# Twenty short chunks in the state-space scan of a hybrid encoder layer, and a new order of the work around it

## The chip, the core and the metric

One core of a Trainium2 chip runs the whole program in one launch. The metric is device microseconds of one execution, as the median of three runs. A core has five engines with queues of their own: TensorE (PE, matmuls; its weight loads are shown as PEld), VectorE (DVE), ScalarE (ACT), GpSimd (POOL) and SyncE (SP), which here issues nearly all DMAs. Each engine runs its instructions in the order of its queue.

## The reference

One layer of an encoder on 256 + 1024 tokens of width 1024. The input projection feeds three mixers; then come an output projection, a gated MLP, a gated layer embedding and a final norm. The change is about the second mixer, S5: 16 groups of 64 complex states, one recurrence forward and one backward, each from `s_t = a s_(t-1) + B u_t`:

```python
bu_re = jnp.einsum('blgi,gpi->blgp', ug, bb_re)
bu_im = jnp.einsum('blgi,gpi->blgp', ug, bb_im)
_, _, s_re, s_im = lax.associative_scan(
    complex_linear_combine, (a_re, a_im, bu_re, bu_im), reverse=rev, axis=1)
y_dir = jnp.einsum('blgp,gip->blgi', s_re, cr) - jnp.einsum('blgp,gip->blgi', s_im, ci)
```

The first mixer, SSD, is a chunked scan over x, B and C, which a projection, a width-3 convolution and SiLU make (`xbc`); it needs step sizes dt and their running sums (`dt_prep`).

## The kernel before

Everything is kept with features on the 128 partitions and tokens along the free axis. A product in near-float32 is three matmuls of high and low parts; `wload` loads a weight block of 128 columns, ScalarE rounds it (`whi`), and VectorE or GpSimd makes the rest (`wlo`, L70).

*S5.* Eight tokens make one block, so there are 32 + 128 = 160 blocks. `s5_coef` makes the coefficients and their powers up to 8. `s5_fac` makes, for four groups at a time, the factors `v1p` (VectorE, L1085 to L1090), which PE transposes (`ps_v`, L1095) and ScalarE copies out (L1096), and `wc` (GpSimd, L1103 to L1107), both stored to DRAM; 64 small matmuls give the taps inside a block (`ps_k`, L1111). `s5_pow` makes the table Q of the first 32 powers of a^8. `s5_scan` multiplies the factors with the blocks (`ps_w`, L1232; two groups at a time, eight times) and copies the result out of PSUM into S (L1236 to L1239), forward states on partitions 0 to 63, backward ones reversed on 64 to 127. S is [component, 16 groups x 5 chunks, 33]: 160 blocks are five chunks of 32, the first chunk the short sequence. Then the recurrence runs over j = 2 to 32 inside all chunks at once: four instructions a step (L1250 to L1253), VectorE on groups 0 to 10 (2 x 11 x 5 = 110 elements) and GpSimd on groups 11 to 15 (50 elements). The ends of chunks are carried to the next (L1267 and the same four lines), and each block gets the power times the state that enters its chunk: twelve pairs of a product (L1280) and a sum (L1281) on each engine. `s5_taps` stores the taps. `s5_out` copies the states before each block into X (L1304 to L1307, VectorE) and multiplies (`ps_y`, L1318 and L1320).

*What sets the order.* Functions are generators. `xbc` issues 8 projection blocks, each 3 windows of 24 matmuls of about 430 columns (`ps_i`, L468), with a `yield` after every six: 96 steps of some 1.07 us of planned time. `drive` steps the main generator and lets a `Background` go on whenever planned time has passed its own wait; `finish` issues all that is left. That gives the order of issue, which is the priority: a planner with a timeline of its own then lays each engine's queue, taking the first instruction that it holds to be ready. The work on a finished window (`flush`: three VectorE instructions L397, L679 and L681, two of ScalarE, one store) and weight loads get high priority.

Before the change `s5_fac` and `s5_pow` are issued whole, ahead of `xbc`. Then the first 72 steps of `xbc` run with `s5_scan` behind a wait of 16 us and `dt_prep` from the start; the other 24 steps run beside `ssd1` (L1610), which needs the stored x and B and `dt_prep`'s weights; then two z blocks (`gate`, 24 steps) run beside `ssd1` and `s5_out`, and everything of these is finished (L1616) before the other two z blocks. Buffers are stacks of pools: `dt_prep`'s (`dtw`) are on the right side, S (`s5s`) on the left.

Of the kernel before, what the change touches and what calls it, by code (L numbers as in the profile page):

```python
# [1141 lines left out]
def s5_pow(k):  # L1142
    v = k.nc.vector
    t = lambda nm, sh: k.s5w.tile([128] + sh, F32, name="s5_" + nm)

# [7 lines left out]
    Q = k.s5p.tile([128, 2, 32, 16], F32, name="s5_Q")
    v.tensor_copy(out=Q[:, :, 0], in_=k.s5P[:, :, 8])
    TQ = t("TQ", [2, 16, 16])
    for n in (1, 2, 4, 8, 16):
        j = signed(f"qj{n}", Q[:, 1, n - 1])
        bc = lambda a: a.unsqueeze(1).to_broadcast([128, n, 16])
        for c in range(2):
            v.tensor_tensor(out=TQ[:, c, :n], in0=bc(j[:, c]), in1=Q[:, 1 - c, 0:n], op=ALU.mult)  # L1160
            v.tensor_tensor(out=Q[:, c, n:2 * n], in0=bc(Q[:, 0, n - 1]), in1=Q[:, c, 0:n], op=ALU.mult)
        v.tensor_tensor(out=Q[:, :, n:2 * n], in0=Q[:, :, n:2 * n], in1=TQ[:, :, :n], op=ALU.add)
    k.s5q = Q
    k.s5j8 = signed_p(k, Q[:, 1, 0], "s5_j8")
    k.s5j256 = signed_p(k, Q[:, 1, 31], "s5_j256")
# [38 lines left out]
def s5_scan(k):  # L1204
    nc = k.nc
    k.s5xd = k.s5ud.rearrange("t (i g) b -> (t i) g b", g=16)

# [55 lines left out]
    tc_ = k.s5s.tile([128, 2, 2, 16], F32, name="s5_tc")
    sh = [128, 2, 16]
    a256 = Q[:, 0, 31].unsqueeze(1).to_broadcast(sh)
    for c in range(2, 5):
# [564 lines left out]
```

## Time and profile before

| what | us |
|---|---|
| median of 3 runs (1745.33 to 1749.23) | 1746.09 |
| the profiled execution, its own time | 1741.83 |
| its span, first to last instruction | 1740.0 |
| PE busy (94%) | 1633.0 |
| DVE busy (63%) | 1097.3 |
| ACT busy (48%) | 832.4 |
| POOL busy (47%) | 825.3 |
| 84 to 340 us: PE / DVE / POOL busy, of 256 | 229.3 / 236.2 / 116.5 |

Busy time is the time covered by an engine's instructions. Matmuls are pipelined, so a busy PE isn't PE at its peak, and the granted clock has to be read beside it. Most of the span, from 560 us on, is the MLP, where PE is nearly always busy. The stretch of the change is 84 to 340 us.

### The profile page before, as it was taken

Reading aid. Unit: us, or ns where it says so; the run is one execution under the profiler, and the core shown is the slowest. Engines: PE = TensorE matmul, PEld = TensorE weight load, DVE = VectorE, ACT = ScalarE, POOL = GpSimd, SP = SyncE. Lnnn points to the kernel's source line nnn. Section 1 sums busy time; section 2 is a strip of 40 time slices with the busy share of each in tenths; the row PEclk is TensorE's granted clock in tenths of the full one; section 3 lists DMA queues with packets and bytes.
Section 4 is the critical chain, followed back from the end, with each engine's and each line's share of the span. In section 5 each row is a group of like instructions: output and inputs, shape, how many; then the busy total and the mean of one; then the engine's idle time right before and its main releaser. Section 6 shows DMA issues by size and latency. Waiting matters only on the chain.

```text
span 1740.0 us, 27569 instructions
## 1 busy us (share of the span) xinstructions
PE 1633.0 (94%) x10384; PEld 1565.3 (90%) x10384; DVE 1097.3 (63%) x2053; ACT 832.4 (48%) x1363; POOL 825.3 (47%) x514
## 2 busy tenths in 40 slices
PE   6979988999888999999999999999999999999995
PEld 4869976887678998999999999999999999999994
DVE  8996999858698988345755521655543465553255
ACT  5323422167556565545655533555543455554353
POOL 5251575167584655744444444444454434444333
PEclk9989999999988999999999999999999999999997
DMA  6535345797885548755444444444466434444443
GB/s 236 170 139 160 115 131 172 255 298 248 248 266 182 166 147 266 220 184 183 154 134 145 141 136 137 146 145 135 135 191 207 145 126 158 134 145 129 145 142 101
DMA packets 136973, 296.58 MB, mean 170 GB/s; under 512 B 13896, under 2 KB 76296, under 8 KB 136840
## 3 DMA queue, kind: packets, MB, share of 16 engines
q1 hardware_dynamic: 136696, 294.81, 53.1%
q8 instruction: 82, 1.34, 0.3%
q14 instruction: 51, 0.42, 0.1%
q10 hardware_dynamic: 144, 0.00, 0.0%
HBM read 255.02 MB, written 40.80 MB: 170 GB/s over the span
## 4 chain that ended last, share of the span: by engine, by line
PE 66%; DVE 19%; DMA 6%; issue 4%; ACT 2%; POOL 2%; SPq 0%; DVEq 0%; ACTq 0%; POOLq 0%
PE ps_u L78 33%; PE ps_d L271 17%; PE ps_o L78 6%; PE ps_g L78 5%; PE ps_i L468 3%; DMA e<-csd 1%; DVE sgvT L1466 1%; DVE wlo L70 1%; DVE s_S L1252 1%; DMA er<-ecsd 1%; DVE s_S L1253 1%; DVE ic L679 1%; POOL wlo L70 1%; DMA wraw<-in_w_up_dram 1%; DVE ps_i L397 1%
## 5 line engine op out<-in xcount | busy, mean ns | idle before, releaser
L70 POOL TENSOR_TENSOR wlo<-wraw,whi 128x1024 fp32r<-128x1024 f32 (+2 forms) x244 | 583.6, 2394 | 702.1 <-ACT whi L61 699.1
L61 ACT ACTIVATE whi<-wraw 128x1024 fp32r<-128x1024 f32 (+1 forms) x359 | 371.5, 1036 | 420.3 <-issue 170.9
L78 PE MATMUL ps_u<-ahi,whi 128*128 128x342 f32 (+2 forms) x1408 | 440.9, 314 | 7.8 <-DVE cv L186 7.1
L78 PE MATMUL ps_u<-ahi,wlo 128*128 128x342 f32 (+2 forms) x1408 | 438.9, 312 | 0.9 <-POOL wlo L70 0.8
L78 PE MATMUL ps_u<-alo,whi 128*128 128x342 f32 (+2 forms) x1408 | 438.1, 311 | 1.4 <-DVE alo L70 0.8
L78 PEld LDWEIGHTS ps_u<-ahi,whi 128*128 128x128 f32 x1408 | 267.8, 190 | 10.2 <-ACT whi L61 4.9
L78 PEld LDWEIGHTS ps_u<-ahi,wlo 128*128 128x128 f32 x1408 | 269.1, 191 | 2.0 <-POOL wlo L70 1.6
L78 PEld LDWEIGHTS ps_u<-alo,whi 128*128 128x128 f32 x1408 | 268.3, 191 | 2.3 <-DVE alo L70 1.1
L70 DVE TENSOR_TENSOR wlo<-wraw,whi 128x1024 fp32r<-128x1024 f32 (+1 forms) x115 | 144.6, 1258 | 128.8 <-ACT whi L61 128.7
L271 PE MATMUL ps_d<-gh,whi 128*128 128x342 f32 (+2 forms) x704 | 218.8, 311 | 1.2 <-ACT gh L112 1.2
L271 PE MATMUL ps_d<-gh,wlo 128*128 128x342 f32 (+2 forms) x704 | 218.6, 311 | 0.9 <-POOL wlo L70 0.6
L271 PE MATMUL ps_d<-gl,whi 128*128 128x342 f32 (+2 forms) x704 | 218.2, 310 | 0.1
L185 DVE SCALAR_TENSOR_TENSOR cv<-ps_u,c_const,cv 128x341 f32<-128x341 f32 (+2 forms) x176 | 96.3, 548 | 126.6 <-ACT cv L184 126.1
L468 PE MATMUL ps_i<-hi,whi 128*128 128x428 f32 (+5 forms) x408 | 153.7, 377 | 7.8 <-DVE ic L681 4.6
L468 PE MATMUL ps_i<-hi,wlo 128*128 128x428 f32 (+5 forms) x408 | 150.0, 369 | 2.6 <-POOL wlo L70 1.9
L468 PE MATMUL ps_i<-lo,whi 128*128 128x428 f32 (+5 forms) x408 | 150.8, 370 | 0.0
L271 PEld LDWEIGHTS ps_d<-gh,whi 128*128 128x128 f32 x704 | 133.1, 189 | 1.7 <-ACT gh L112 1.4
L271 PEld LDWEIGHTS ps_d<-gh,wlo 128*128 128x128 f32 x704 | 133.3, 190 | 1.3 <-POOL wlo L70 0.8
L271 PEld LDWEIGHTS ps_d<-gl,whi 128*128 128x128 f32 x704 | 133.2, 189 | 0.4 <-DVE gl L70 0.3
L184 ACT ACTIVATE cv<-ps_u,c_const 128x342 f32<-128x342 f32 (+2 forms) x176 | 106.7, 607 | 15.6 <-DVE ps_u L250 15.6
L272 DVE TENSOR_TENSOR x<-ps_d,x 128x342 f32<-128x342 f32 (+2 forms) x32 | 15.7, 492 | 152.1 <-PE ps_d L271 152.1
L186 DVE SCALAR_TENSOR_TENSOR cv<-ps_u,c_const,cv 128x341 f32<-128x341 f32 (+2 forms) x176 | 96.3, 548 | 3.7
(428 smaller groups left out, 2956.5 us busy)
## 6 DMA issues: line engine op xcount, KB each, us to landing
wraw<-in_w_up_dram SPq DMA_DIRECT2D x176, 512.0 KB, 3.3
wraw<-in_w_down_dram SPq DMA_DIRECT2D x64, 512.0 KB, 3.5
wraw<-in_w_out_dram SPq DMA_DIRECT2D x32, 512.0 KB, 3.9
wraw<-in_ple_gate_dram SPq DMA_DIRECT2D x32, 512.0 KB, 3.4
...
```

The lines of the kernel that those rows point to most:

```text
L61: nc.scalar.activation(out=hi[:, :n], in_=raw[:, :n], func=AF.Copy)
L70: eng.tensor_tensor(out=lo, in0=x, in1=hi.bitcast(F32), op=ALU.subtract)
L78: k.nc.tensor.matmul(out=out, lhsT=a, rhs=b, start=(i == 0 and j == 0), stop=(i == n - 1 and j == 2))
L184: nc.scalar.activation(out=c[:, :N], in_=ps[:, :N], func=AF.Identity, scale=cw[:, 1:2], bias=cb)
L185: nc.vector.scalar_tensor_tensor(out=c[:, 1:N], in0=ps[:, 0:N - 1], scalar=cw[:, 0:1], in1=c[:, 1:N], op0=ALU.mult, op1=ALU.add)
L186: nc.vector.scalar_tensor_tensor(out=c[:, 0:N - 1], in0=ps[:, 1:N], scalar=cw[:, 2:3], in1=c[:, 0:N - 1], op0=ALU.mult, op1=ALU.add)
L271: nc.tensor.matmul(out=ps[:, :N], lhsT=a[:, i], rhs=g[f][r][:, :N], start=(f == 0 and j == 0), stop=(f == NF - 1 and j == 2))
L397: k.nc.vector.tensor_tensor(out=ps if out is None else out, in0=ps, in1=k.rstd[:n, a:b], op=ALU.mult)
L468: nc.tensor.matmul(out=ps, lhsT=x[:, i], rhs=k.h[i][y][:, a:b], start=i + n == 0, stop=i == KC - 1 and n == 2)
L679: nc.vector.scalar_tensor_tensor(out=o(s, b), in0=u(s - 1, b - 1), scalar=k.scw[:, j, 0:1], in1=o(s, b), op0=ALU.mult, op1=ALU.add)
L1252: e.tensor_tensor(out=dst, in0=dst, in1=t[:, 0], op=ALU.add)
L1253: e.tensor_tensor(out=dst, in0=dst, in1=t[:, 1], op=ALU.add)
```

## The change

The scan's chunks become 8 blocks long, 20 of them: 4 for the short sequence, 16 for the long one. S becomes [component, 9, 16 groups, 20 chunks], j outside; the recurrence has 7 steps; VectorE takes groups 0 to 11 and GpSimd 12 to 15. The chunk ends are scanned in two levels (within fours, then four times from one four to the next, with the table R of powers of a^64), copied to j = 0, and the correction is made with 8 products and 8 sums for 7 x n x 20 elements, n = 6 twice on VectorE and 4 once on GpSimd. Evictions are two copies an engine instead of three; of X's four VectorE copies one stays and two go to ScalarE. `s5_fac` gets yields and runs, behind a wait of 7 us, beside the first 40 steps of `xbc`, and `dt_prep` behind a wait of 20 us; both are finished there. `s5_pow` follows, `dtw` is closed on the left, where `s5s` is then opened, and `s5_scan` runs beside the next 32 steps without a wait of its own.

```diff
         v.tensor_tensor(out=v1[:, 1], in0=v1[:, 1], in1=tm[:, 1], op=ALU.add)
+        yield 6
...
         nc.sync.dma_start(out=k.s5wc[q4], in_=w)
+        yield 5
...
+    TQ = t("TQ", [2, 4, 16])
+    k.s5q = powers("Q", k.s5P[:, :, 8], 8, TQ)
+    k.s5r = powers("R", k.s5q[:, :, 7], 4, TQ)
+    k.s5j8 = signed_p(k, k.s5q[:, 1, 0], "s5_j8")
...
-    S = k.s5s.tile([128, 2, 80, 33], F32, name="s5_S")
-    k.s5F, k.s5S = S, S.rearrange("p c (g k) j -> p c g k j", g=16)
+
+    S = k.s5S = k.s5s.tile([128, 2, 9, 16, 20], F32, name="s5_S")
...
-            copy(out=S[0:64, c, 5 * g0:5 * g0 + 5 * n, 1:33], in_=src[0:64].rearrange("p g (c j) -> p (g c) j", j=32))
-            o = k.s5S[64:128, c, g0:g0 + n]
-            copy(out=o[:, :, 0, 1:33], in_=src[64:128, :, 31::-1])
-            copy(out=o[:, :, 1:5, 1:33], in_=src[64:128, :, :31:-1].rearrange("p g (c j) -> p g c j", j=32))
+            for h, s in ((0, src[0:64]), (64, src[64:128, :, ::-1])):
+                copy(out=S[h:h + 64, c, 1:9, g0:g0 + n].rearrange("p j g q -> p g q j"), in_=s.rearrange("p g (q j) -> p g q j", j=8))
...
-    parts = ((nc.vector, 0, 11), (nc.gpsimd, 11, 16))
...
-    for j in range(2, 33):
+
+    for j in range(2, 9):
...
+            mac(e, t, S[:, :, j, g0:g1], ar, aj, S[:, :, j - 1, g0:g1])
+
+    E = S[:, :, 8]
+    v = nc.vector
+    t4 = flat[0][:, :320].rearrange("p (i c g q) -> p i c g q", i=2, c=2, q=5)
+    for i in range(1, 4):
+        sh = [128, 2, 16, 5]
+        mac(v, t4, E[:, :, :, i::4], R[:, 0, 0].unsqueeze(1).unsqueeze(3).to_broadcast(sh), jr[:, :, 0].unsqueeze(3).to_broadcast(sh), E[:, :, :, i - 1::4])
+    for m in range(1, 5):
+        p = slice(64 if m == 1 else 0, 64 if m == 4 else 128)
+        sh = [p.stop - p.start, 2, 16, 4]
+        ar = R[p, 0].rearrange("p i g -> p g i").unsqueeze(1).to_broadcast(sh)
+        mac(v, t4[p, :, :, :, 0:4], E[p, :, :, 4 * m:4 * m + 4], ar, jr[p].rearrange("p c i g -> p c g i"), E[p, :, :, 4 * m - 1:4 * m].to_broadcast(sh))
+    v.memset(S[:, :, 0, :, 0:1], 0.0)
+    v.tensor_copy(out=S[:, :, 0, :, 1:20], in_=E[:, :, :, 0:19])
+    v.memset(S[0:64, :, 0, :, 4:5], 0.0)
+    v.memset(S[64:128, :, 0, :, 16:17], 0.0)
+
+    for e, g0, g1 in ((nc.vector, 0, 6), (nc.gpsimd, 12, 16), (nc.vector, 6, 12)):
...
+        sh = [128, 7, n, 20]
+        t = flat[e is nc.gpsimd][:, :140 * n].rearrange("p (j g q) -> p j g q", j=7, q=20)
+        q = [Q[:, m, 0:7, g0:g1].unsqueeze(3).to_broadcast(sh) for m in range(2)]
+        en = [S[:, m, 0, g0:g1].unsqueeze(1).to_broadcast(sh) for m in range(2)]
+        for m, a, b, op in ((0, 0, 0, ALU.add), (0, 1, 1, ALU.subtract), (1, 0, 1, ALU.add), (1, 1, 0, ALU.add)):
+            o = S[:, m, 1:8, g0:g1]
+            e.tensor_tensor(out=t, in0=q[a], in1=en[b], op=ALU.mult)
+            e.tensor_tensor(out=o, in0=o, in1=t, op=op)
...
-        nc.vector.tensor_copy(out=X[0:64].rearrange("p c g (k j) -> p c (g k) j", j=32), in_=k.s5F[0:64, :, 5 * g0:5 * g0 + 10, 0:32])
-        nc.vector.tensor_copy(out=X[64:128, :, :, 31::-1], in_=S[64:128, :, g0:g0 + 2, 0, 0:32])
+        nc.vector.tensor_copy(out=X[0:64].rearrange("p c g (q j) -> p c (g q) j", j=8), in_=S[0:64, :, 0:8, g0:g0 + 2].rearrange("p c j g q -> p c (g q) j"))
         for c in range(2):
-            nc.vector.tensor_copy(out=X[64:128, c, :, :31:-1].rearrange("p g (k j) -> p g k j", j=32), in_=S[64:128, c, g0:g0 + 2, 1:5, 0:32])
+            nc.scalar.copy(out=X[64:128, c, :, ::-1].rearrange("p g (q j) -> p g q j", j=8), in_=S[64:128, c, 0:8, g0:g0 + 2].rearrange("p j g q -> p g q j"))
...
-    s5_fac(k)
+
+    d = ExitStack()
+    open_(d, "dtw", 1)
+    open_(d, "dtw2", 1)
+    g1, g2 = Background(wait(7), s5_fac(k)), Background(wait(20), dt_prep(k))
+    xs = xbc(k)
+    drive(k, islice(xs, 40), g1, g2)
+    finish(g1, g2)
     s5_pow(k)
+    d.close()
     b.close()
     open_(a, "s5s", 1)
     open_(a, "s5o", 2)
-    b = ExitStack()
-    open_(b, "dtw", 1, side="right")
-    open_(b, "dtw2", 1, side="right")
-    g1, g2 = Background(wait(16), s5_scan(k)), Background(dt_prep(k))
-    xs = xbc(k)
-    drive(k, islice(xs, 72), g1, g2)
-    finish(g2)
-    b.close()
+    g1 = Background(s5_scan(k))
+    drive(k, islice(xs, 32), g1)
```

## Rows read from the trace of the kernel before

**Rows 1.** Busy by stretch: start:end length, PE, PEld, DVE, ACT, POOL, clock, DMA.
```profile
84.00:130.00 46.00, 34.64 (x184) 29.91 (x183) 44.74 (x74) 9.90 (x14) 27.85 (x17) 0.85 0.36 128
130.00:200.00 70.00, 70.00 (x385) 65.21 (x383) 55.65 (x165) 27.22 (x54) 11.51 (x14) 1.00 0.47 149
200.00:340.00 140.00, 124.65 (x622) 106.12 (x623) 135.80 (x305) 30.17 (x47) 77.15 (x150) 0.98 0.53 168
```

**Rows 2.** The same for the projection's matmuls (L468) alone: PE, PEld, clock, DMA.
```profile
84.00:200.00 116.00, 69.31 (x320) 61.16 (x319) 0.94 0.43 141
130.00:200.00 70.00, 49.68 (x239) 44.64 (x240) 1.00 0.47 149
200.00:340.00 140.00, 93.63 (x420) 78.42 (x419) 0.98 0.53 168
```

**Rows 3.** Waits of PE, 84 to 340 us: total, times, longest.
```profile
PE ps_v L1095 <- DVE v1p L1089: 10.5, 3, 3.9
...
PE ps_bT L756 <- DVE bT L778: 8.3, 6, 2.4
```

**Rows 4.** DVE's groups of the scan: busy us, mean ns, idle before.
```profile
L1250 DVE TENSOR_TENSOR s_t<-s_Q,s_S 128x110 f32<-128x110 f32 x31 | 11.6, 373 | 0.4
...
L1251 DVE TENSOR_TENSOR s_t<-s_j,s_S 128x110 f32<-128x110 f32 x31 | 13.1, 424 | 0.0
...
L1252 DVE TENSOR_TENSOR s_S<-s_S,s_t 128x110 f32<-128x110 f32 x31 | 16.7, 539 | 0.0
...
L1253 DVE TENSOR_TENSOR s_S<-s_S,s_t 128x110 f32<-128x110 f32 x31 | 14.3, 461 | 0.3
...
L1280 DVE TENSOR_TENSOR s_tE<-s_Q,s_S 128x352 f32<-128x352 f32 x12 | 9.9, 824 | 0.1
...
L1281 DVE TENSOR_TENSOR s_S<-s_S,s_tE 128x352 f32<-128x352 f32 x12 | 8.6, 718 | 0.1
```

**Rows 5.** Instructions on S alone, 181 to 310 us: DVE, ACT, POOL busy.
```profile
181.00:310.00 129.00, 76.38 (x167) 1.78 (x6) 63.82 (x148) 0.97 0.45 143
```

**Rows 6.** Instructions on S: shortest/median/longest ns, first and last start.
```profile
L1250 DVE TENSOR_TENSOR s_t<-s_Q,s_S x31: 342/361/522, 181.5 to 269.0; 128x110 f32<-128x110 f32 x31
...
L1252 DVE TENSOR_TENSOR s_S<-s_S,s_t x31: 299/465/2325, 182.2 to 271.6; 128x110 f32<-128x110 f32 x31
...
L1253 DVE TENSOR_TENSOR s_S<-s_S,s_t x31: 297/365/1450, 182.9 to 273.1; 128x110 f32<-128x110 f32 x31
...
L1280 DVE TENSOR_TENSOR s_tE<-s_Q,s_S x12: 741/774/1028, 274.0 to 308.5; 128x352 f32<-128x352 f32 x12
...
L1281 DVE TENSOR_TENSOR s_S<-s_S,s_tE x12: 508/524/2033, 275.7 to 309.3; 128x352 f32<-128x352 f32 x12
...
L1281 POOL TENSOR_TENSOR s_S<-s_S,s_tE x12: 491/582/847, 275.2 to 297.5; 128x160 f32<-128x160 f32 x12
...
L1307 DVE COPY s5X<-s_S x16: 285/289/292, 307.2 to 337.2; 64x256 f32<-64x256 f32 x16
```

**Rows 7.** Timeline of DVE, alone and beside POOL: start us, us, instruction.
```profile
83.62 1.59 DVE L1087 TENSOR_TENSOR v1p<-s_PW,s_bba 128x512 f32<-128x512 f32 x1
...
102.50 0.69 DVE L1087 TENSOR_TENSOR v1p<-s_PW,s_bba 128x512 f32<-128x512 f32 x1
...
203.19 2.33 DVE L1252 TENSOR_TENSOR s_S<-s_S,s_t 128x110 f32<-128x110 f32 x1
```

**Rows 8.** Timeline of POOL in the last of these moments.
```profile
202.90 2.39 POOL L70 TENSOR_TENSOR wlo<-wraw,whi 128x1024 fp32r<-128x1024 f32 x1
```

**Rows 9.** Timeline of DVE: start and end of `dt_prep`, last eviction.
```profile
155.93 0.33 DVE L595 TENSOR_TENSOR dtx<-ps_dtT,c_const 128x160 f32<-128x160 f32 x1
...
191.68 0.47 DVE L1236 COPY s_S<-ps_w 64x320 f32<-64x320 f32 x1
...
209.54 0.39 DVE L565 TENSOR_TENSOR lncs<-sl_y,csc 128x160 f32<-128x160 f32 x1
```

More of the change, by code (lines that the diff above doesn't have):

```diff
@@ L1111, in s5_fac @@
                 nc.tensor.matmul(out=pk[32 * q4:32 * q4 + 32, 128 * s:128 * s + 128], lhsT=bd[:, c, g + s], rhs=w[:, c, s], start=c == 0, stop=c == 1)
+    yield 1
     kt = k.s5k.tile([128, 4, 128], F32, name="s5_kt")
     nc.scalar.activation(out=kt, in_=pk.rearrange("p (s e) -> p s e", s=4), func=AF.Copy)
+    yield 2
     p0 = k.psb.tile([128, 512], F32, tag="psb", name="ps_k0")
@@ L1117, in s5_fac @@
     nc.tensor.matmul(out=p0[:, :64], lhsT=k.sel1, rhs=kt[:, :, 112:128], start=False, stop=True)
+    yield 1
     dd = k.s5k.tile([128, 4, 16], F32, name="s5_dd")
@@ L1150, in signed, with powers @@
         return j
[L1153 to L1165, printed above, removed]
+    def powers(nm, first, n_, T):
+        Q = k.s5p.tile([128, 2, n_, 16], F32, name="s5_" + nm)
+        v.tensor_copy(out=Q[:, :, 0], in_=first)
+        n = 1
+        while n < n_:
+            j = signed(f"{nm}j{n}", Q[:, 1, n - 1])
+            bc = lambda a: a.unsqueeze(1).to_broadcast([128, n, 16])
+            for c in range(2):
+                v.tensor_tensor(out=T[:, c, :n], in0=bc(j[:, c]), in1=Q[:, 1 - c, 0:n], op=ALU.mult)
+                v.tensor_tensor(out=Q[:, c, n:2 * n], in0=bc(Q[:, 0, n - 1]), in1=Q[:, c, 0:n], op=ALU.mult)
+            v.tensor_tensor(out=Q[:, :, n:2 * n], in0=Q[:, :, n:2 * n], in1=T[:, :, :n], op=ALU.add)
+            n *= 2
+        return Q
+    TQ = t("TQ", [2, 4, 16])
+    k.s5q = powers("Q", k.s5P[:, :, 8], 8, TQ)
+    k.s5r = powers("R", k.s5q[:, :, 7], 4, TQ)
+    k.s5j8 = signed_p(k, k.s5q[:, 1, 0], "s5_j8")
+    k.s5jr = k.s5p.tile([128, 2, 4, 16], F32, name="s5_jr")
+    v.tensor_scalar(out=k.s5jr[:, 0], in0=k.s5r[:, 1], scalar1=-1.0, scalar2=None, op0=ALU.mult)
+    v.tensor_copy(out=k.s5jr[:, 1], in_=k.s5r[:, 1])
 def signed_p(k, a, nm):
@@ L1242, in s5_scan, with mac @@
         yield 1
-    S = k.s5S
-    Q, j8, j256 = k.s5q, k.s5j8, k.s5j256
-    parts = ((nc.vector, 0, 11), (nc.gpsimd, 11, 16))
-    tmp = [k.s5s.tile([128, 2, 2, g1 - g0, 5], F32, name=f"s5_t{g0}") for _, g0, g1 in parts]
-    def mac(e, t, dst, ar, aj, src, n):
+    Q, j8, R, jr = k.s5q, k.s5j8, k.s5r, k.s5jr
+    parts = ((nc.vector, 0, 12), (nc.gpsimd, 12, 16))
+    flat = [k.s5s.tile([128, n], F32, name=f"s5_t{n}") for n in (960, 560)]
+    tmp = [f[:, :80 * (g1 - g0)].rearrange("p (i c g q) -> p i c g q", i=2, c=2, q=20) for f, (_, g0, g1) in zip(flat, parts)]
+    def mac(e, t, dst, ar, aj, src):
         e.tensor_tensor(out=t[:, 0], in0=ar, in1=src, op=ALU.mult)
@@ L1263, in s5_scan @@
[L1263 to L1266, printed above, removed]
-        nc.vector.tensor_copy(out=S[:, :, :, c, 0], in_=S[:, :, :, c - 1, 32])
-        if c > 2:
-            mac(nc.vector, tc_, S[:, :, :, c, 0], a256, j256, S[:, :, :, c - 1, 0], 1)
-    parts2 = ((nc.vector, 0, 11), (nc.gpsimd, 11, 16))
-    for (e, g0, g1) in parts2:
-        n = g1 - g0
-        for c in range(2, 5):
-            t = k.s5s.tile([128, n, 32], F32, tag=f"s5_tE{g0}", name="s5_tE")
-            sh = [128, n, 32]
-            qr = Q[:, 0, :, g0:g1].rearrange("p j g -> p g j")
-            qi = Q[:, 1, :, g0:g1].rearrange("p j g -> p g j")
-            en = lambda m: S[:, m, g0:g1, c, 0].unsqueeze(2).to_broadcast(sh)
-            for m, q, a, op in ((0, qr, 0, ALU.add), (0, qi, 1, ALU.subtract), (1, qr, 1, ALU.add), (1, qi, 0, ALU.add)):
-                e.tensor_tensor(out=t, in0=q, in1=en(a), op=ALU.mult)
-                e.tensor_tensor(out=S[:, m, g0:g1, c, 1:33], in0=S[:, m, g0:g1, c, 1:33], in1=t, op=op)
+            mac(e, t, S[:, :, j, g0:g1], ar, aj, S[:, :, j - 1, g0:g1])
```

4 lines of the change are left out of this document (1 added, 3 removed).

## The prediction

> **What bounds the kernel now.** I first cut the span into stretches and read the busy time of every engine. The change touches 84 to 340 us, where the projection of x, B and C (`ps_i` of `xbc`), the state-space factors, the scan, the step sizes, `ssd1` and the first two z blocks run. The reader is to see in [rows 1] that TensorE (PE), which bounds the kernel elsewhere, isn't full here: it is idle 11.4 us of 84 to 130, 0 of 130 to 200 and 15.4 of 200 to 340, 26.7 us together. In 84 to 130 its granted clock is 0.85, so it spent about 30% of the stretch at 1.2 GHz instead of 2.4: up to 6.9 us more, and by the same reckoning up to 2.8 us after 200. PE can give back 27 to 37 us and no more. VectorE (DVE) is busy 44.7 of 46 us at first, 55.7 of 70 then, and 135.8 of 140 at last. In the first and the third stretch DVE is the bound, and PE waits for it: the waits of PE [rows 3] name `v1p` (10.5 us, made by `s5_fac`) and `bT` (8.3 us, made by `ssd1`, whose copy stands in DVE's queue among the scan's instructions).
>
> What fills DVE after 181 us is the scan [rows 4]: 31 steps of four instructions on 110 elements, 11.6 + 13.1 + 16.7 + 14.3 = 55.7 us, and 24 instructions of 352 elements for the correction, 18.5 us; with some 4 us for the carries it is 78 us, of which 70 fall after 200. GpSimd (POOL) does its share beside it, 63.8 us [rows 5].
>
> **The change, part by part.**
> *Shorter scan.* With chunks of 8 blocks instead of 32 there are 7 steps instead of 31, each on 20 chunks instead of 5, and q is now the innermost, contiguous index. The 28 DVE instructions hold 2 x 12 x 20 = 480 elements. Undisturbed durations from [rows 6, 7]: 512 contiguous elements 0.69 us, 352 contiguous 0.508, the same 352 with a strided factor 0.741, 110 strided 0.342. So 480 contiguous take 0.65: 28 x 0.65 = 18.2 us. The correction has 16 DVE instructions of 7 x 6 x 20 = 840 elements; from 352 to 512 the slope is 1.1 ns an element, so 1.02 us each: 16.3 us. Between them is a part that is new in kind: 12 instructions of 160 strided elements (0.42 by the strided row) and 16 of 128 (0.3), with one copy and memsets: 11 us. Sum 45.5 us.
>
> To that comes what POOL does to it. In [rows 7] a 512-element product takes 0.69 us alone and 1.59 where POOL works on products of the same size; a 110-element sum took 2.33 us across a 2.39 us POOL split [rows 8]. In the scan the DVE means [rows 4] stand over the minima [rows 6] by 0.03, 0.08 (the shape of the row before it), 0.24 and 0.16 us, 0.51 a step or 16 us in all, and 3.5 us in the correction: 19.5 us for 63.8 us of POOL. After the change POOL has 28 instructions of 160 elements (0.49, [rows 6]) and 8 of 560 (about 1.3 by the 160 row and the 512 ones): 25 us. At the scan's own rate DVE pays 25 x 0.31 = 8 us, at that of the 512-element pairs, whose instructions are long like the new ones (0.9 us for 1.56 of POOL), 14 us; bounds 0 and 25. I take 12.5, nearer to the second: 58 us, bounds 45.5 to 70.5. The scan costs DVE 78 - 58 = **20 us less** (8 to 33).
>
> The Trainium skill states for this ("SBUF — State Buffer", section "Who interferes with whom") that a DVE instruction with two SBUF inputs and a GpSimd instruction that reads SBUF hold their common port exclusively, the other fully blocked for the whole instruction. By that DVE would pay for all of POOL's 25 us (the second rival below); the 2.33 us sum agrees, the scan's average of 0.31 doesn't.
>
> *Evictions and reads of the states.* S is now written and read with j as the outer index, so these copies stride by 320 elements. A strided factor costs (741 - 508) / 352 = 0.66 ns an element [rows 6]. Eviction: three DVE copies a pair of groups become two of 320, each 0.47 us if contiguous [rows 9] and 0.68 if strided, against 1.1 us for the three: -1.4 to +2 us over eight pairs, taken as 0. X: DVE gives two copies of 0.29 us [rows 6] and a shorter one to ScalarE, some 5 us over eight pairs, and pays 0.4 to 0.7 us more for the strided one that it keeps: -2 to +1 us, taken as -1. ScalarE gets 16 copies of some 0.5 us, 8 us, in 200 to 340 where it is busy 30 of 140 [rows 1]; PE's `ps_y` then waits for ScalarE's queue too, whose longest other instruction there is a weight split of about 1 us.
>
> *Powers.* `s5_pow` loses its two longest levels and gains a short table of four, 41 small instructions in all. It comes before the scan, where DVE has room (55.7 of 70): nothing on the path, bounds 0 and some us of a later scan.
>
> *Factors spread over `xbc`.* The same 24 DVE products, 20 POOL ones, 32 transposes and 64 small matmuls are issued, and the same eight DMAs, now 6 and 5 us of planned time apart. So PE has blocks of x between a `v1p` and the transposes that need it, and DVE no longer runs its products beside POOL's. I let the 11.4 us of idle time and 4 of the 6.9 us of slow clock go, and keep 5 us of new gaps: 84 to 130 loses about 10 us. SP's queue: the stores of the two factors now stand among weight loads and `xbcd` stores; each is issued after its DVE, POOL or ScalarE producer, and the weight load behind it is needed a block (15 us) later. The step sizes move 20 us later with their one weight-sized load, which takes one of two weight buffers for a block, as it does now.
>
> *Scan issued later.* It now follows 40 + 18 = 58 of the 96 steps of `xbc`, instead of about 34. When does it start? Before the last `ps_w` PE must do 57 steps of six matmuls. At full clock [rows 2] gives 49.68 / 239 = 0.208 us each: 71.1 us. All other PE work before 200 us is 104.6 - 69.3 = 35.3 us [rows 1, 2], the same as then. 84 + 71.1 + 35.3 + 5 of gaps = 195. There is a new wait: S lies where the buffers of `dt_prep` were, so the first eviction waits for `lncs`. Today that chain of some 60 small DVE instructions runs from 155.9 to 209.9 us, among the scan's instructions [rows 9]. It will start at about the same time (its last `ps_dtT` comes after some 40 steps, 159 us) and has no scan beside it: 60 x 0.33 us, and a third more for the conv of `xbc`, puts `lncs` at 186. Eight groups at 2.5 us, mostly DVE's and ScalarE's copies, follow: S is loaded at **206 us**, against 192 now [rows 9].
>
> *Sum.* At 206 PE has done some 66 steps of `xbc`, against 53 at 200 today (320 matmuls, [rows 2]), and 13 steps are 6 us of conv on DVE. So DVE then has 135.8 - 70 + 58 - 1 - 6 = 117 us before it, and 2 us idle: 325. PE has from 195 on 63 steps (78.6 us) and the 31 us of other work of [rows 1, 2] (124.65 - 93.63): 305 to 308. DVE is still the bound, but as PE is ahead, the last 6 us of DVE's backlog run under the third z block: the second one ends in effect at 319 instead of 340, and the rest shifts: **21 us less**. The profiled execution took 1741.8 us (span 1740.0), 4.3 under the median of the runs, 1746.1. So 1720.8 in such an execution, **1725 us** as a median.
>
> **Rivals.**
> *PE becomes the bound.* DVE may finish `ssd1` and `s5_out` under the third and fourth z block; then PE's 305 to 308 decides, and the gain is the 32 to 37 us that PE can give at all: 1711. For it: the full 130 to 200. Against it: `ssd1` makes PE wait for DVE chunk by chunk.
> *The port takes most of it back.* DVE pays for all of POOL's 25 us: 70.5 us for the scan, 12.5 more, gain 8: 1738. The 1.59 us products speak for it, the scan's average against it.
> *It doesn't do what it says (no change).* The order that runs is by readiness: DVE takes the products of `s5_fac` as soon as it is free, so the spreading is void (10 us back), and the later scan with `ssd1` close behind turns the other 11 us into waits for `bT` and `xw`: 1746.
> *Slower: the scan starts too late.* One mechanism: S waits for the log of the step sizes. DVE does conv meanwhile, so the price is about 0.55 us for each us, and it decides from 186 + 21 / 0.55 = 224 us on. If the chain, issued 20 us later, starts at 180 and takes the 54 us that it takes now, `lncs` is at 234 and S at 254: 5 us slower, and `ssd1` with `s5_out` behind it add some us of PE waits: 1754. For it: the chain's present length. Against it: what stretches it now is the scan itself.
>
> **How the numbers follow.** Forecast 0.50, PE bound 0.18, port 0.12, no change 0.10, slower 0.10. The forecast's own range is 1715 to 1735 (the scan's bounds on DVE and a few us of its start). For 8 in 10 I take 1705 to 1743: it holds the first three and part of the fourth. 0.2% is 3.5 us, about what a measurement of this kernel can tell. Faster: 0.50 + 0.18 + 0.12 = 0.80; same 0.10; slower 0.10.
>
> **What would show it.** Right: PE's wait for `v1p` under 3 us and a clock over 0.93 in the first 46 us of `xbc`; 28 DVE steps of 0.65 to 1.0 us and 16 corrections of 1.0 to 1.5, the scan 53 to 63 us on DVE; last eviction at 198 to 214 us; DVE still over 95% busy from there on; third z block starting at 310 to 328. Wrong: first eviction after 200; steps over 1.2 us (port); PE idle under 5 us after 200 (PE bound); or as much more idle time in 340 to 560 as was saved before it.

## The result: half a per cent slower

The changed kernel takes 1755.87 us (median of 4 runs, 1754.52 to 1757.04), the kernel before, run beside it, 1746.00: ratio 1.0051, 95% interval 1.0032 to 1.0071. I had forecast 1725. Its profiled execution took 1757.04 us, with a span of 1755.2 us, 15.2 more than that of the kernel before, whose profiled execution was a quick one (1741.83). One execution of e17 below took 2654 us, half as long again as all others, and is left out of its median.

Busy time by stretch in the changed kernel (columns as in [rows 1]):

```profile
84.00:130.00 46.00, 39.85 (x213) 36.92 (x211) 37.46 (x96) 13.21 (x19) 23.42 (x16) 0.93 0.35 121
130.00:200.00 70.00, 70.00 (x383) 64.62 (x382) 51.70 (x110) 22.00 (x33) 13.84 (x8) 1.00 0.39 128
200.00:340.00 140.00, 133.24 (x703) 117.38 (x702) 128.62 (x224) 49.57 (x75) 52.37 (x47) 1.00 0.56 175
340.00:560.00 220.00, 174.53 (x1104) 152.29 (x1103) 163.75 (x239) 117.90 (x271) 127.91 (x72) 0.86 0.78 241
560.00:640.00 80.00, 72.60 (x576) 69.91 (x575) 67.79 (x118) 54.84 (x97) 42.23 (x21) 0.98 0.54 172
```

The two later stretches of the kernel before:

```profile
340.00:560.00 220.00, 191.31 (x1266) 170.80 (x1261) 163.13 (x253) 137.51 (x302) 137.85 (x75) 0.93 0.84 254
560.00:640.00 80.00, 76.07 (x637) 73.83 (x635) 74.15 (x126) 49.41 (x87) 45.40 (x22) 1.00 0.46 149
```

Up to 340 us the change does for PE what was forecast. It is idle 12.9 us of the 256 instead of 26.7 [rows 1], and the clock stands at 0.93, 1.00 and 1.00 instead of 0.85, 1.00 and 0.98. Then it is all given back. From 340 to 560 PE is idle 45.5 us instead of 28.7, at a mean clock of 0.86 instead of 0.93; from 560 to 640 it is idle 7.4 instead of 3.9. By idle time and clock deficit (length times what the clock lacks to 1), PE gains 20.3 us ahead of 340 and loses 37.3 from 340 to 640: 17 us net, for a span that is 15.2 longer.

What PE waits for, 84 to 340 us, the two rows that answer to [rows 3]:

```profile
PE ps_i L468 <- DVE s5up L1198: 6.2, 1, 6.2
PE ps_bT L756 <- DVE bT L778: 3.9, 4, 1.8
```

The wait for `v1p` is gone, `bT` costs 3.9 us instead of 8.3, and one wait of 6.2 us for `s5up` is new.

DVE's groups of the scan, which answer to [rows 4]:

```profile
L1299 DVE TENSOR_TENSOR s_t<-s_Q,s_S 128x840 f32<-128x840 f32 x8 | 11.5, 1443 | 0.0
L1300 DVE TENSOR_TENSOR s_S<-s_S,s_t 128x840 f32<-128x840 f32 x8 | 10.2, 1276 | 0.1
...
L1262 DVE TENSOR_TENSOR s_t<-s_Q,s_S 128x480 f32<-128x480 f32 x7 | 7.0, 995 | 0.9 <-ACT s_S L1251 0.8
...
L1263 DVE TENSOR_TENSOR s_t<-s_j,s_S 128x480 f32<-128x480 f32 x7 | 5.6, 803 | 0.0
L1264 DVE TENSOR_TENSOR s_S<-s_S,s_t 128x480 f32<-128x480 f32 x7 | 5.0, 712 | 0.0
L1265 DVE TENSOR_TENSOR s_S<-s_S,s_t 128x480 f32<-128x480 f32 x7 | 4.9, 694 | 0.1
```

28 steps take 7.0 + 5.6 + 5.0 + 4.9 = 22.5 us, the 16 corrections 21.7; with 12.8 us for the part between them (28 small instructions, a copy, memsets) it is 57.0 us. The scan on DVE is as short as forecast (58). But it doesn't run when it was forecast to. Timeline of DVE, answering to [rows 9]: start of `dt_prep`'s chain, its end, the first eviction of S, the first step of the scan, the last eviction:

```profile
159.10 0.31 DVE L595 TENSOR_TENSOR dtx<-ps_dtT,c_const 128x160 f32<-128x160 f32 x1
...
203.76 0.32 DVE L565 TENSOR_TENSOR lncs<-sl_y,csc 128x160 f32<-128x160 f32 x1
...
209.33 1.45 DVE L1251 COPY s_S<-ps_w 64x320 f32<-64x320 f32 x2
...
236.27 0.66 DVE L1262 TENSOR_TENSOR s_t<-s_Q,s_S 128x480 f32<-128x480 f32 x1 [0.82 <-ACT s_S L1251]
...
248.82 1.47 DVE L1251 COPY s_S<-ps_w 64x320 f32<-64x320 f32 x2
```

S, the array of the states, is loaded at 250.3 us, not at 206. And DVE, which saved 21 us of scan, pays for that with idle time. DVE is the third pair in these rows; first before, then after:

```profile
84.00:236.00 152.00, 136.07 (x713) 123.59 (x711) 135.88 (x316) 45.94 (x81) 72.70 (x109) 0.94 0.40 129
236.00:340.00 104.00, 93.21 (x474) 77.65 (x476) 100.31 (x227) 21.35 (x34) 43.82 (x72) 0.98 0.61 195
```

```profile
84.00:236.00 152.00, 145.85 (x799) 136.19 (x798) 115.06 (x250) 55.77 (x83) 39.63 (x24) 0.98 0.45 145
236.00:340.00 104.00, 97.24 (x498) 82.73 (x497) 102.73 (x178) 29.01 (x45) 49.99 (x46) 1.00 0.51 164
```

From 84 to 236 us DVE has 115.1 us of work instead of 135.9: 20.8 us more in which it stands idle because the scan isn't there yet (of work on S it has 8.8 us there instead of 40.9, of all other work 106.3 instead of 95.0). From 236 on it is full in both (100.3 and 102.7 of 104). So about as much as the scan saves was lost ahead of it, and everything that needs DVE after it comes no earlier.

What then starts late is `ssd2`, the last pass of the SSD mixer, which takes ten chunks one after the other, loads x, B and C of each (`xbc`) and multiplies them (`ps_G`). This work on PE, before and after (the last two times are first and last start):

```profile
L882 PE MATMUL ps_G<-xbc x40: 272/275/377, 351.0 to 499.8; 128*128 128x128 f32 x40
```

```profile
L882 PE MATMUL ps_G<-xbc x40: 272/275/423, 367.2 to 524.0; 128*128 128x128 f32 x40
```

It starts 16.2 us later (367.2), its last chunk comes 24 us later, and the time is 9.9 us longer. The input projection itself (`ps_i`, L468) is through 35 us earlier: the last of its matmuls starts at 434 us instead of 469. So fewer of them are left to fill PE's waits beside `ssd2`; I call this spent cover, or used-up blocks, below.

### The profile page after: what moved, and what is told of

Read it like the earlier page. It is cut to its first block, busy times and chain, and to the rows that moved or that the text cites. A ratio compares the mean times of both kernels' runs of the same rounds, so it can differ in the third digit from the quotient of the medians.

```text
span 1755.2 us, 27358 instructions
## 1 busy us (share of the span) xinstructions
PE 1641.9 (94%) x10384; PEld 1575.2 (90%) x10384; DVE 1087.0 (62%) x1938; ACT 844.8 (48%) x1368; POOL 791.9 (45%) x402
## 4 chain that ended last, share of the span: by engine, by line
PE 61%; DVE 14%; DMA 5%; issue 3%; ACT 3%; POOL 1%; SPq 0%; DVEq 0%; ACTq 0%; POOLq 0%
PE ps_u L78 31%; PE ps_d L271 17%; PE ps_o L78 5%; PE ps_g L78 5%; PE ps_i L468 1%; DMA xbc<-xbcd 1%; DMA e<-ed 1%; DVE wlo L70 1%; DMA wraw<-in_w_up_dram 1%; POOL wlo L70 1%; DVE alo L236 1%; DVE s_t L1299 1%; DVE xw L781 1%; DVE acc L179 1%; DVE sgvT L1484 0%
## 5 line engine op out<-in xcount | busy, mean ns | idle before, releaser
L468 PE MATMUL ps_i<-hi,whi 128*128 128x428 f32 (+5 forms) x408 | 150.9, 370 | 10.4 <-DVE s5up L1198 6.2
L468 PE MATMUL ps_i<-lo,whi 128*128 128x428 f32 (+5 forms) x408 | 149.5, 366 | 0.0
L468 PE MATMUL ps_i<-hi,wlo 128*128 128x428 f32 (+5 forms) x408 | 148.0, 365 | 0.5 <-POOL wlo L70 0.5
L184 ACT ACTIVATE cv<-ps_u,c_const 128x342 f32<-128x342 f32 (+2 forms) x176 | 106.7, 607 | 19.8 <-DVE ps_u L250 19.8
```

Source lines behind the costliest of these rows:

```text
L184: nc.scalar.activation(out=c[:, :N], in_=ps[:, :N], func=AF.Identity, scale=cw[:, 1:2], bias=cb)
L468: nc.tensor.matmul(out=ps, lhsT=x[:, i], rhs=k.h[i][y][:, a:b], start=i + n == 0, stop=i == KC - 1 and n == 2)
```

## The experiments

In all of them the first start of `ps_G` is read as above, from one profiled execution. The kernel before is run beside each (1743.8 to 1746.5 us).

| run | first `ps_G` | median us | ratio, interval |
|---|---|---|---|
| before | 351.0 | 1746.0 | |
| after | 367.2 | 1755.9 | 1.0051 (1.0032 to 1.0071) |
| e1 new scan, old order | 341.4 | 1744.5 | 0.9993 (0.9981 to 1.0006) |
| e2 old scan, new order | 398.1 | 1783.5 | 1.0218 (1.0198 to 1.0238) |
| e3 `dtw` moved | 365.6 | 1754.4 | 1.0051 (1.0037 to 1.0065) |
| e4 yd from POOL | 368.9 | 1751.3 | 1.0034 (1.0023 to 1.0045) |
| e5 before, scan late | 366.4 | 1755.7 | 1.0064 (1.0044 to 1.0085) |
| e6 after, no correction | 347.8 | 1738.0 | 0.9963 (0.9951 to 0.9976) |
| e7 e1, no correction | 335.4 | 1736.0 | 0.9949 (0.9930 to 0.9968) |
| e8 before, less PE | 362.5 | 1737.8 | 0.9961 (0.9948 to 0.9974) |
| e9 scan at step 24 | 360.3 | 1754.7 | 1.0060 (1.0043 to 1.0077) |
| e10 e1, `ssd1` faster | 352.6 | 1750.8 | 1.0037 (1.0024 to 1.0050) |
| e11 e1, scan earlier | 341.6 | 1746.0 | 1.0000 (0.9988 to 1.0013) |
| e12 e10 + e11 + e4 | 354.5 | 1746.0 | 0.9999 (0.9986 to 1.0013) |
| e13 before, `ssd2` late | 367.5 | 1760.1 | 1.0075 (1.0063 to 1.0087) |
| e14 after, z 12 | 365.0 | 1756.6 | 1.0054 (1.0041 to 1.0066) |
| e15 e1, z 12 | 346.3 | 1746.7 | 0.9999 (0.9987 to 1.0010) |
| e16 after, less PE | 364.4 | 1741.5 | 0.9973 (0.9962 to 0.9984) |
| e17 `dt_prep` stores from POOL | 369.4 | 1759.0 | 1.0068 (1.0055 to 1.0081) |

### The two halves of the change, alone (e1, e2)

```diff
 e1: the changed kernel's scan with
+    finish(Background(s5_fac(k)))
+    s5_pow(k)
...
+    g1, g2 = Background(wait(16), s5_scan(k)), Background(dt_prep(k))
+    drive(k, islice(xs, 72), g1, g2)
 e2: the old scan, powers and copies with the changed kernel's order
     (a scratch tile of the powers moved into a buffer of the factors)
```

> The new scan, powers, evictions and reads of the states, in the order of the kernel before (factors ahead of xbc, scan after 16 us of it, dt_prep beside it). Theory (late scan): S is loaded by about 195 us as before, the scan is some 20 us shorter on DVE, its last correction ends near 290 instead of 309, ssd2's first load comes at 322 to 330 instead of 341, and the time is 1728 to 1738. Rival (the new instructions themselves cost it: strided evictions, strided reads on ACT, corrections): no faster than before, 1746 to 1756. Rival (spent cover: whatever PE gains ahead of 340 is missing as cover for ssd2): 1742 to 1748, with more idle PE time in 340 to 560.

> The new order (factors and dt_prep spread over 40 steps of xbc, then the scan) around the old scan of 32-block chunks. Theory (late scan): S is loaded near 250 as in the changed kernel, the scan of 78 us on DVE ends near 355, ssd2's first load comes near 380, and the time is 1768 to 1785, more than 10 us above the changed kernel. Rival (new instructions): the order alone gives its PE time back, 1730 to 1742. Rival (spent cover): about as the changed kernel, 1750 to 1760.

e2 came as the late scan has it: S is loaded at 259 us, `ssd2` starts 47 us after that of before, and the time is 38 us longer. So the new order alone loses 38 us, and the shorter scan inside it takes 28 of these back.

```profile
L882 PE MATMUL ps_G<-xbc x40: 272/275/421, 398.1 to 535.9; 128*128 128x128 f32 x40
```

e1 missed the theory's 1728 to 1738: 1744.5, no difference from before. The number is that of the third theory, spent cover. Its stretches:

```profile
84.00:236.00 152.00, 136.19 (x721) 123.06 (x720) 137.51 (x279) 51.74 (x75) 59.53 (x51) 0.96 0.41 133
236.00:340.00 104.00, 100.57 (x527) 87.39 (x527) 85.36 (x157) 32.33 (x50) 27.83 (x17) 1.00 0.69 218
340.00:560.00 220.00, 186.82 (x1264) 167.86 (x1262) 165.41 (x251) 133.24 (x293) 138.37 (x75) 0.91 0.80 242
```

Early on DVE is as full as before (137.5 us up to 236), and the scan's saving is seen from 236 to 340, where DVE has 85.4 us of work instead of 100.3. But that frees DVE, and nothing else: `ssd2` starts 9.6 us earlier, PE's idle time falls from 26.7 us to 19.2 in 84 to 340, and rises again, 28.7 to 33.2 us, in 340 to 560, at a clock of 0.91 instead of 0.93. Here a start 9.6 us earlier than that of the kernel before was worth nothing.

### Is it the late scan? (e5, e13)

```diff
 e5, in the kernel before:
-    Background(wait(16), s5_scan(k))
+    Background(wait(40), s5_scan(k))
 e13, in the kernel before:
-    Background(wait(4), ssd2(k))
+    Background(wait(20), ssd2(k))
```

> The kernel before, with the scan started after 40 us of xbc in the plan instead of 16; nothing else is changed, the factors are still made ahead of xbc. Theory (ssd2's start decides once it is later than about 341 us): S is loaded some 25 us later (near 218), ssd2's first load comes at 350 to 365 and the time rises by 0.8 us for each us of that, to 1753 to 1765, although PE is not slowed. Rival (the time is lost by the spread factors or by the new instructions, not by the scan's start): 1744 to 1749.

> The kernel before with nothing changed but ssd2's start: issued after 20 us of the remaining z steps instead of 4. Scan, factors, ssd1 and PE's projection as before. Theory (ssd2's start carries the loss): first load near 355 instead of 341 and a time 0.6 to 0.8 us longer for each us of it, 1753 to 1759. Rival (ssd2's start is a symptom; the loss comes from DVE's work on the scan or from PE's used-up blocks alone): 1744 to 1749.

e5 came as the theory has it. It has the old scan, the old order, nothing of the change. It only loads S later, 178 to 220 us instead of 149 to 192, here by its first DVE copies:

```profile
L1236 DVE COPY s_S<-ps_w x8: 469/473/477, 178.1 to 219.8; 64x320 f32<-64x320 f32 x8
```

```profile
L882 PE MATMUL ps_G<-xbc x40: 270/275/421, 366.4 to 527.7; 128*128 128x128 f32 x40
```

That alone makes 12 us, as much as the changed kernel loses (9.9), with the same start of `ssd2` (366.4 and 367.2). e13 leaves the scan as it is and issues only `ssd2` later. Its first load isn't moved (341.7 us), against what I expected; its second is (355.3 instead of 347.3), and so is its first work on PE:

```profile
L882 PE MATMUL ps_G<-xbc x40: 272/275/579, 367.5 to 547.0; 128*128 128x128 f32 x40
```

```profile
200.00:340.00 140.00, 125.42 (x616) 107.62 (x615) 136.49 (x306) 30.61 (x48) 77.45 (x150) 0.96 0.52 167
340.00:560.00 220.00, 186.79 (x1244) 168.39 (x1244) 155.55 (x233) 125.33 (x273) 123.53 (x70) 0.93 0.77 240
```

Ahead of 340 us it is like the kernel before (PE 125.4 busy, DVE 136.5, against 124.7 and 135.8 in [rows 1]), `ssd2` starts 16.5 us later and the time is 13.6 us longer, 1 us over the range expected. Three kernels, with different reasons for it, start `ssd2` at 366 to 368 us and take 1755.7 to 1760.1. By the medians, the price of a later start is 0.6 (after), 0.8 (e2, e5, e13: 38 / 47, 12 / 15, 13.6 / 16.5) us for each us; by the profiled executions it is 0.9 to 1.1.

That isn't a law. Among the other kernels that do the whole computation and start `ssd2` over 5 us later than before, the price goes from 0.3 (e4) to 0.9 (e9). And e13 can't tell a late start from used-up blocks: while `ssd2` waits, PE goes on with the projection, so that 288 of its matmuls are left at the first `ps_G`, against 368 in the kernel before and 190 in the changed one.

### How much does DVE's work, and PE's, count? (e6, e7, e8, e16)

```diff
 e6 in the changed kernel, e7 in e1: no correction
-            e.tensor_tensor(out=t, in0=q[a], in1=en[b], op=ALU.mult)
-            e.tensor_tensor(out=o, in0=o, in1=t, op=op)
 e8 in the kernel before, e16 in the changed one: two products of three in xbc
+            part = ((hi, 0), (hi, 1)) if 6 <= j < 14 else ((hi, 0), (hi, 1), (lo, 0))
```

> The changed kernel without the correction of the scan (16 DVE and 8 POOL instructions left out, the scan's states stay uncorrected). Theory: S is final some 25 to 35 us earlier (near 300), ssd2's first load comes near 335 to 340, and of the 22 us of DVE work taken away 12 to 16 come off the time: 1740 to 1744, as the kernel before. Rival (cover spent: what is lost is PE's work ahead of 340, whatever DVE does): 1750 to 1756.

> The new scan in the old order, also without the correction. Theory (an ssd2 that starts earlier than in the kernel before gives nothing more, because 420 to 640 us takes it back): ssd2's first load at 310 to 320 instead of 331, but a time of 1740 to 1745, at most 4 us under the same kernel with the correction. Rival (DVE work ahead of 340 counts everywhere alike): 15 us less, 1728 to 1732.

> The kernel before, with the projection of x, B and C cut to two of its three products (low half of the weights left out): 192 matmuls, some 39 us of PE, gone ahead of 250 us, the plan of the order unchanged. Theory (DVE and the chain to ssd2 set the end of this part, PE's lead is worth nothing): ssd2's first load within 5 us of 341 and a time of 1740 to 1746. Rival (PE's position in the projection sets the end, as my prediction had it): 1712 to 1725.

> The changed kernel with the projection of x, B and C cut to two of its three products (low half of the weights left out), some 39 us of PE gone, as e8 did to the kernel before, which gained 6. Theory (DVE and the chain to ssd2 set the end, PE's lead is worth next to nothing): ssd2's first load within 5 us of 359, 1748 to 1756. Rival (PE's place in the projection still counts): 1725 to 1740.

Compared by their ratios, in the changed kernel the 21.7 us of correction on DVE (with POOL's share of it) are worth 15 us (1.0051 to 0.9963), within the theory's 12 to 16 (the time, 1738.0, is 2 us under its range), and `ssd2` starts 3 us ahead of that of the kernel before:

```profile
L882 PE MATMUL ps_G<-xbc x40: 270/275/421, 347.8 to 504.6; 128*128 128x128 f32 x40
```

In the old order (e7) the same work is worth 8 us (0.9993 to 0.9949), between what the theory (at most 4) and its rival (15) had. Two things follow. The new order costs 38 us with the old scan (e2), 10 with the new one (e1 against the changed kernel) and 2, within the intervals, without the correction (e7 against e6): it costs more the more work DVE still has to do when S is late. And e6 has only 232 matmuls of the projection left at its first `ps_G`, against 368 in the kernel before, and is faster than it: used-up blocks alone aren't the loss.

Some 39 us of PE work taken away are worth 7 us in the kernel before, and 14 in the changed one, where I had expected at most 8; both times lie between the theory's range and the rival's. In the changed kernel:

```profile
L883 PE MATMUL ps_G<-xbc x40: 270/275/421, 364.4 to 512.1; 128*128 128x128 f32 x40
```

There `ssd2` starts only 2.8 us earlier than in the changed kernel, and yet the time is 14 us shorter. In e8 it even starts 11.5 us later than in the kernel before (first load at 352.5 us, where I expected 341), and the time is 7 us shorter. So its start isn't all that counts, and PE's work isn't worth nothing: 0.17 and 0.35 us for each us, against 0.7 for DVE's in the changed kernel. Why it counts more there, and why `ssd2` starts late in e8, no run shows.

### Why is the scan late? (e3, e9, e17)

```diff
 e3:
-    open_(d, "dtw", 1)
+    open_(d, "dtw", 1, side="right")
 e9: e3 and
-    drive(k, islice(xs, 40), g1, g2)
+    drive(k, islice(xs, 24), g1, g2)
...
-    drive(k, islice(xs, 32), g1)
+    drive(k, islice(xs, 48), g1)
 e17: e3 and, in dt_prep, for csd and ecsd
-        nc.sync.dma_start(...)
+        nc.gpsimd.dma_start(...)
```

> The changed kernel with dt_prep's two pools on the other side of the memory, so that S doesn't lie over them and the first eviction needs not wait for lncs and the stores of ecsd. Theory (late scan): first eviction about 10 us earlier (near 199 instead of 208.7), S loaded near 240, ssd2 5 to 10 us earlier, time 1747 to 1752. Rivals: first eviction is paced by PE's order and not by the buffers, or the scan's time doesn't matter: 1754 to 1757.

> The changed kernel with dt_prep's pools on the other side (as in e3) and the scan issued after 24 steps of xbc instead of 40: what is left of the factors and of dt_prep at that point is issued at once. Theory (ssd2 starts when DVE and ssd1/s5_out are through, and the scan is late because the order issues it late, not because of a buffer): first eviction near 185, S loaded near 228 instead of 250, ssd2's first load at 342 to 350, time 1743 to 1749. Rival (the spreading itself costs, or the scan's place doesn't matter): 1753 to 1757.

> e3 (dt_prep's pools out of S's way) with dt_prep's six stores of csd and ecsd issued from POOL's queue instead of SP's. If SP's order is what holds the scan's first loads until dt_prep is through, they come 10 to 20 us earlier (185 to 194 instead of 203.4), S is loaded at 230 to 240, ssd2's first PE work comes some 8 us earlier and the time falls to 1745 to 1751. If the planned place of the whole scan holds it (it is issued after 40 steps and after dt_prep, on every engine), the loads stay within 4 us of 203 and the time at 1753 to 1757.

e3 decides against my step "S lies over the buffers of `dt_prep`": with the overlap gone, the first load of the scan's input still comes at 203.4 us (203.8 with it), directly behind `dt_prep`'s stores in SP's queue:

```profile
201.29 1.51 SPq L659 DMA_DIRECT2D ecsd<-cst  x2
202.92 0.40 SPq L683 DMA_DIRECT2D xbcd<-ic  x1
203.37 0.93 SPq L1231 DMA_DIRECT2D s5x<-s_ud  x2
```

e17 takes these stores out of SP's queue. The load then comes at 206.2, not earlier (the time, 1759.0, is 2 us over the range for this case, which no row explains):

```profile
205.23 0.96 SPq L734 DMA_DIRECT2D xb<-xbcd  x2
206.23 1.02 SPq L1231 DMA_DIRECT2D s5x<-s_ud  x2
```

So neither the buffers nor these stores hold it; what is left is the place that the planner gave the scan, which is issued after `dt_prep` and the factors. e9 moves that place by 16 steps, and the load comes 15 us earlier (188.3). The evictions start at 196.4 instead of 209.3 and end 11 us earlier (239 us, where I had expected 228). `ssd2` starts at 360.3, 6.9 us earlier, with its first load at 347 as expected; but the time stays at 1754.7, where 0.8 us for each us would give 1750. So e9 missed the theory's 1743 to 1749 and fell into the range of its rival: that the spreading itself costs, or that the scan's place doesn't matter. Against the second half of the rival stands e5, where the scan's place alone makes 12 us. The first half stays open: in e9 the rest of the factors and of `dt_prep` is issued at once ahead of the scan. Its profiled execution, at 1760.2 the slowest of six, has PE idle 17.0 us from 340 to 420, against 11.0 in the changed kernel, and no row names one cause.

### What else stands ahead of `ssd2`? (e4, e10, e11, e12, e14, e15)

In the changed kernel SP's queue holds three stores of `s5_out` for 8.1 us directly ahead of the first load of `ssd2`:

```profile
351.25 8.12 SPq L1344 DMA_DIRECT2D s_yd<-s5y  x3
359.43 0.53 SPq L800 DMA_DIRECT2D xbc<-xbcd  x1
```

```diff
 e4, in s5_out, for yd (L1344):
-        nc.sync.dma_start(...)
+        nc.gpsimd.dma_start(...)
 e10 in e1:
-    Background.hop = 2
+    Background.hop = 1
 e11 in e1:
-    Background(wait(16), s5_scan(k))
+    Background(wait(8), s5_scan(k))
 e14 in the changed kernel, e15 in e1:
-    drive(k, islice(z, 24), g2, s1)
+    drive(k, islice(z, 12), g2, s1)
-    Background(wait(4), ssd2(k))
+    Background(wait(16), ssd2(k))
```

> The changed kernel with the eight stores of s5_out (yd) issued from POOL's queue instead of SP's, where three of them stand for 8.1 us directly ahead of ssd2's first loads. If SP's order holds ssd2 back, its first load comes 5 to 8 us earlier (351 to 354 instead of 359.4) and the time falls by 3 to 8 us to 1748 to 1753. If it is the buffers of S and X below, or s5_out's end itself, the load stays within 2 us of 359 and the time at 1755 to 1757.

> The new scan in the old order (as e1), with ssd1's and s5_out's steps issued 1 us of planned time apart instead of 2. If ssd1's pace (a chunk each 9 us from 241 on) rather than DVE sets ssd2's start there, ssd1 ends near 305 instead of 323, ssd2's first load comes at 315 to 322 and the time is 1735 to 1741. If DVE sets it: as e1, 1743 to 1746.

> The new scan in the old order with the scan started after 8 us of xbc in the plan instead of 16. S loaded some 8 to 10 us earlier (near 183) and its last correction near 282. Theory (in the old order the scan's end no longer decides; e7 took all of the correction away and gained 8): 1741 to 1745. Rival (each us of an earlier scan counts, as each us of a later one did at 0.7 to 0.8): 1736 to 1739.

> e10 and e11 together, and the stores of yd from POOL's queue as in e4. If ssd2's start still carries some time, all three move it to 305 to 318 and the time is 1731 to 1739; if 420 to 640 us takes everything back, 1742 to 1746 with more idle PE time there.

> The changed kernel with twelve instead of 24 steps of z issued beside s5_out and the rest of ssd1, so that 36 are left for ssd2 (whose start is put off by 16 us of the plan from there, so it comes 3 steps earlier against z than now). If used-up projection blocks are a second cause, more of them stand beside ssd2, 260 to 300 matmuls at its start instead of 211, and the time falls to 1744 to 1751. If ssd2's start alone decides, its first load stays at 355 to 360 and the time at 1753 to 1757.

> The same edit on the new scan in the old order (e1). Used-up blocks as a cause: 1736 to 1741. ssd2's start alone: as e1, 1742 to 1747.

e4: the load comes at 351.6 instead of 359.4, but the chunk's first matmuls no earlier (368.9). 1751.3 us fall into the range expected, but the intervals of e4 and of the changed kernel overlap, so at most a few us hang on that queue. e10 went the wrong way: `ssd1` ended only 5 us earlier (318 instead of 323), `s5_out` 11 us later, `ssd2` 11 us later, and the time is 6 us over e1. e11 brought nothing, as expected. e12 is no better than e1. e14 and e15 tell nothing of their question: the planner laid the queues so that about the same number of projection matmuls stands behind `ssd2`'s first load (211 in e14 as in the changed kernel, 376 in e15 against 407 in e1). Whether the used-up blocks add a loss of their own stays open.

No version that does the whole computation beats the kernel before.

## Why the prediction was wrong

*Factors spread.* Right. 84 to 130 loses 5.2 us less by idle time and 3.7 by the clock (0.93 instead of 0.85), 8.9 against "about 10"; the wait for `v1p` went. That DVE would no longer run its products beside POOL's didn't come: the first four, from 80.7 us on, still take 1.5 to 1.6 us each beside POOL's products, much as before.

*Scan on DVE.* Right: 57.0 us against 58. Undisturbed it is 45.5 us as worked out (the shortest durations are 0.65 us for a step and 1.02 for a correction), and POOL's share costs 11.5 (12.5 forecast), for 33.8 us of POOL on S instead of 25: 0.34 us for each us of POOL, nearly the 0.31 of before. Single instructions stretch much more: a product of the correction takes up to 2.72 us. The Trainium skill's rule that the other engine "fully blocks" for the whole instruction ("SBUF — State Buffer", "Who interferes with whom") would, if DVE paid for all of POOL's work at its shortest durations (26.5 us), by an estimate make it 45.5 + 26.5 = 72 us. The sum in this trace, 57.0, does not agree; the single stretched instructions do. Instructions on S alone, before and after (columns as in [rows 5]):

```profile
84.00:360.00 276.00, 93.62 (x216) 7.17 (x24) 63.82 (x148) 0.96 0.52 167
```

```profile
84.00:360.00 276.00, 73.80 (x100) 23.13 (x32) 33.78 (x36) 0.99 0.48 155
```

Scan, evictions and copies together, DVE has 19.8 us less of work on S; 21 had been forecast.

*Copies.* Evictions cost DVE 11.6 us, against 8 x (0.474 + 0.227 + 0.420) = 9.0 before: +2.6, over the end of my range (+2). X costs 6.9 us against 5.9 + 1.8 + 4.6 = 12.3 before (L1304, L1305, L1307), 5.4 less instead of 1 less; 2.1 us of that are one copy that took 2.58 us before. The strided copy that DVE keeps costs 0.37 us more than the contiguous one (0.86 and 0.485), just under the forecast's 0.4 to 0.7, and the copies that it gave away had cost 6.4 us, not "some 5". Together the copies are no dearer than forecast, and they aren't what decides. The rows, first X before, then DVE and ScalarE after (duration shortest/median/longest, first and last start):

```profile
L1305 DVE COPY s5X<-s_S x8: 224/224/224, 269.6 to 336.1; 64x128 f32<-64x128 f32 x8
L1304 DVE COPY s5X<-s_S x8: 475/485/2578, 310.4 to 335.6; 64x640 f32<-64x640 f32 x8
```

```profile
L1251 ACT COPY s_S<-ps_w x16: 707/730/745, 208.7 to 246.8; 64x320 f32<-64x320 f32 x16
L1251 DVE COPY s_S<-ps_w x16: 708/728/740, 209.3 to 249.6; 64x320 f32<-64x320 f32 x16
...
L1299 DVE TENSOR_TENSOR s_t<-s_Q,s_S x8: 1016/1247/2720, 297.8 to 332.1; 128x840 f32<-128x840 f32 x8
L1300 DVE TENSOR_TENSOR s_S<-s_S,s_t x8: 1020/1036/2114, 299.4 to 335.0; 128x840 f32<-128x840 f32 x8
L1323 DVE COPY s5X<-s_S x8: 842/858/894, 319.6 to 351.0; 64x640 f32<-64x640 f32 x8
```

*Scan issued later.* This is the step that failed. "S is loaded at 206" had two mis-sized terms. `dt_prep`'s chain began as forecast (159.1 us, "some 40 steps, 159"), but took 44.7 us instead of 27, and the evictions began at 209.3. In that time DVE gave 15.3 us to `xbc`'s windows, where the third that I had added allows 7, and 3.6 us to the rest of the factors, which I had not counted. The windows, 159 to 204.1 us:

```profile
L679 DVE SCALAR_TENSOR_TENSOR ic<-ps_i,c_const,ic 128x426 f32<-128x426 f32 (+2 forms) x8 | 5.2, 655 | 0.0
L681 DVE SCALAR_TENSOR_TENSOR ic<-ps_i,c_const,ic 128x428 f32<-128x428 f32 (+1 forms) x8 | 5.2, 655 | 0.0
L397 DVE TENSOR_TENSOR ps_i<-ps_i,rstd 128x430 f32<-128x430 f32 (+2 forms) x8 | 4.9, 607 | 1.1 <-PE ps_i L468 1.1
```

So the rival's argument against a long chain, that the scan stretches it, was wrong too: without a scan beside it the chain takes 45 us instead of 54. Nor is it the buffer of `lncs` that the evictions wait for, as the step has it (e3): by e9 they come when the plan issues them, behind `dt_prep`. And "eight groups at 2.5 us" took 41 us: 5.1 us each, and more at the end. That number could have been read. The kernel before spends 43 us on the same eight groups (the row gives the first copy of each):

```profile
L1236 DVE COPY s_S<-ps_w x8: 472/474/483, 149.4 to 191.7; 64x320 f32<-64x320 f32 x8
```

I counted what DVE and ScalarE need for the copies and left out that each group waits for its turn among PE's projection blocks, the work of `xbc`'s windows on DVE and its own loads; [rows 9] shows only the last eviction. With 41 us the forecast would have been S at 227 from my own end of that chain, and 250 from the real first eviction. The slower rival has 254 us for S, 0.55 us for each us of delay and 1754: its mechanism (S waits for the log of the step sizes) fell with e3 and e17, and that its place and its time came out so near is in part luck. It had a chance of 0.10.

*"As PE is ahead ... the rest shifts."* Wrong as well, and it would have been wrong with S on time: e1 has S at 192 us, a scan that is as short, PE 7.5 us less idle ahead of 340, and no gain. PE's lead isn't what the next part waits for. `ssd2` is issued when `ssd1` and `s5_out` are through, and a later start of it, with the cover that is spent meanwhile, costs (e13). The prediction's last sign of being wrong, "as much more idle time in 340 to 560 as was saved before it", is what the profile shows: 16.8 us more, against 13.8 saved.

Open: why an earlier start than 351 us is worth nothing with the whole computation (e1, e11) and 8 us without the correction (e7), why an earlier scan inside the new order brings nothing (e9), how much of the price of a late `ssd2` is its start and how much the spent cover (e13), and why PE's work counts more in the changed kernel (e16).
